# Layer B's attention: 128 joined logits per query, value differences, and the first units laid among eight gate tiles

## The chip, the cores and the metric

The kernel runs on one core of a Trainium2 chip. The metric is the device time of one execution in microseconds (us), lower is better. The kernel before takes 2511.83 us, the median of 3 runs (2511.45 to 2513.24).

## The reference

A trunk of two layers over 2048 positions of width 1024. Layer A projects, attends causally with a forgetting bias, gates and projects out. From its output the keys and values of 4 heads are computed once. Layer B projects 16 query heads and a gate, attends over a window of 128 positions with one learned sink per head, multiplies by silu(gate) and projects out. The change lies in layer B. Its attention, for blocks of 128 queries and a band of 256 keys (the block's own 128 and the 128 before them):

```python
diff = (jnp.arange(WINDOW)[:, None] + WINDOW) - jnp.arange(2 * WINDOW)[None, :]
in_window = (diff >= 0) & (diff < WINDOW)
...
logits = jnp.where(valid[None, :, None, None], logits, -jnp.inf)
sink = jnp.broadcast_to(sinks.astype(jnp.float32).reshape(1, 1, hkv, g, 1, 1), logits.shape[:-1] + (1,))
probs = jax.nn.softmax(jnp.concatenate([logits, sink], axis=-1), axis=-1)[..., :-1]
out = jnp.einsum('bnhgqk,bnkhd->bnqhgd', probs.astype(v.dtype), v_band)
...
h = h + (o * jax.nn.silu(gate)) @ w_out_b[j]
```

Of the 256 keys of the band each query sees exactly 128: query q of a block sees keys 0 to q of its own block and keys q+1 to 127 of the block before.

## The kernel before

Names: PE is the matmul engine, DVE the vector engine, ACT the scalar engine (exp, casts), POOL GpSimd, SP the engine that issues DMAs. SBUF is the working memory, PSUM the memory that matmuls write, in banks of 128x512 float32. The kernel holds a float32 number as a high and a low part, both rounded for PE (float32r), so one product is three matmuls where both sides are split.

What runs before the gate's tiles (the first 1957 us) the change leaves as it was, but for small steps on the constants and the norm factors. Layer B runs `projections` (L618), whose last groups are the gate: 2 groups of 16 tiles. A gate tile is 24 matmuls (L715), a DVE product with a row of norm factors (L721), a Silu on ACT (L722) and a DMA to memory. All tiles use the three b2 banks.

Then comes `attention_b` (L1239): 64 units, one for each of 16 query blocks i and 4 key heads g; a unit has 4 query heads. It is a generator, written as slots. Slot n holds, in this order on PE: `scores` of unit n, `weights_t` of unit n-3 (T_LAG_B), 6 matmuls of the output projection, `values` of unit n-4 (V_LAG_B), and 6 more of the projection (`feed`, O_LAG_B 8, FEED_2 6).

- `scores` (L1273): 8 matmuls give the raw logits of 4 heads, 128 queries by 256 keys, in two b2 banks. DVE adds the band mask and takes the maximum, one instruction for each head (L1290), and writes the masked logits to SBUF. DVE computes the negated maximum nm (L1296) and the sink's part es (L1299); ACT takes four exps, one for each head, 256 wide, which also sum up (L1303), and the exp of es (L1300); DVE adds the sum and es (L1307) and takes the reciprocal (L1308); POOL multiplies the 128x1024 weights by it (L1309).
- `weights_t` (L1314): 8 transposes on PE (flip, L343) into two b2 banks, a cast on ACT to the high part ph (L1327), a DVE subtraction for the low part pl (L1328).
- `values` (L1330): 4 matmuls (L1339): two blocks of values, each with ph and pl, into the one pa bank. ACT copies the lower half (L1346), DVE adds the halves (L1348, two instructions), POOL multiplies by the gate (L1352), ACT casts yh (L1354), DVE subtracts yl (L1355).
- `project` (L1361): 24 matmuls (L1374) for each half of a block's output, into the one pb bank; DVE adds the residual from memory (L1379) and a DMA writes the result. 12 matmuls go to each slot, so the add comes every second slot, and the next group cannot start in the bank before that add is done.

Each engine runs its instructions strictly in its own order, which a scheduler has laid down when the program was built. The lags above set which units stand beside each other in it.

A hook in `layer_b` starts the attention's generator inside the last gate group: the load at tile 8, and the slots of the first 6 units (B_AHEAD) among the last 6 tiles. The weights of the output projection are split into high and low parts by `half` (one half, L1157) and, in slots 6 to 9, by `weights` (L411, ACT cast L447 and DVE subtraction L448).

Of the kernel before, what the change touches and what calls it, by code (L numbers as in the profile page):

```python
# [13 lines left out]
F32R = mybir.dt.float32r  # L14
BF16 = mybir.dt.bfloat16
I32 = mybir.dt.int32
# [61 lines left out]
B_AHEAD = 6  # L78
# [67 lines left out]
class Trunk:  # L146
# [56 lines left out]
    def constants(self):  # L203
# [32 lines left out]
        nc.gpsimd.memset(self.band, 0.0)  # L236
        select(self.band[:, 0, :], self.band[:, 0, :], [[1, P]], -1, -1, NEG)
        select(self.band[:, 1, :], self.band[:, 1, :], [[-1, P]], 0, 1, NEG)
# [163 lines left out]
    def rstd_row(self, r, i):  # L402

        nc = self.nc
        ps = self.ps("pa", [NTB, P])
        self.tc.keep_in_program_order(self.flip(ps, r))
        row = self.sb("ro1", [NTB, P])
        nc.vector.tensor_copy(row, ps)
        nc.sync.dma_start(out=self.d["rr"][i].rearrange("(b t) -> b t", t=P), in_=row)
# [208 lines left out]
    def projections(self, normed, groups, row, later=None, pre=None, hook=None, first=None):  # L618
# [75 lines left out]
        for gi, grp in enumerate(groups):  # L694
# [10 lines left out]
            if "gate" in grp:  # L705
                f0, dst = grp["gate"]
                for ch in range(NCH):
                    rows = self.factor_rows(row, ch)
                    for ft in range(CH // P):
                        if hook is not None and gi == len(groups) - 1:  # L710
                            hook(ch * (CH // P) + ft)
                        ps = self.ps("b2", [P, CH])
# [7 lines left out]
                        sg = self.sb("st", [P, CH])  # L720
                        nc.vector.tensor_tensor(sg, ps, rows, ALU.mult)  # L721
                        nc.scalar.activation(sg, sg, AF.Silu)  # L722
# [434 lines left out]
    def half(self, w, i, tag="wr", **more):  # L1157

        bigs = [self.sb("big", [P, 4, 2, CH], F32R) for _ in range(2)]
        return self.weights(  # L1160
            w, i * CH, CH, tag=tag, **more,
            into=lambda p: (bigs[p // 4][:, p % 4, 0, :], bigs[p // 4][:, p % 4, 1, :]),
        )

# [74 lines left out]
    def attention_b(self, w_out, res, dst):  # L1239
# [4 lines left out]
        blk, st = {}, {}  # L1244
# [19 lines left out]
        def load_v(i):  # L1264

            ts_ = slice(i * P, (i + 1) * P)
            v = self.sb(("qn", "qn", "rows")[i % 3], [P, NKV, P], F32R)
            nc.sync.dma_start(
                out=f_(v), in_=d["vb"][:, ts_, :].rearrange("g t e -> t g e")
            )  # L1270
            g = msg[:, 2 + i % 2, :].rearrange("p (c t) -> p c t", t=P)
            nc.sync.dma_start(out=g, in_=d["gtb"][:, ts_].rearrange("(c p) t -> p c t", p=P))
            blk[i][3:5] = v, g  # L1273

        def scores(u):
# [10 lines left out]
            ms = msg[:, u % 2, :].rearrange("p (h k) -> p h k", k=2 * P)  # L1286
            mx = self.sb("mx", [P, G], bufs=6)
            mask = self.band.rearrange("p b k -> p (b k)")[:, 2 * P - w :]
            for h in range(G):
                nc.vector.tensor_tensor_reduce(  # L1290
                    out=ms[:, h, :w], in0=ps[:, h, :w], in1=mask, scale=1.0, scalar=NEG,
                    op0=ALU.add, op1=ALU.max, accum_out=mx[:, h : h + 1],
                )
# [7 lines left out]
            pf = self.sb("st", [P, G, 2 * P])  # L1301
            for h in range(G):
                nc.scalar.activation(  # L1303
                    pf[:, h, :w], ms[:, h, :w], AF.Exp, bias=nm[:, h : h + 1],
# [5 lines left out]
                pf[:, :, :w], pf[:, :, :w], rs.unsqueeze(2).to_broadcast([P, G, w]), ALU.mult  # L1310
# [3 lines left out]
        def weights_t(u):  # L1314

            i, g = units[u]
            nb = blk[i][5] // P
            pf = st[u]
            ps = self.ps("b2", [P, 2, G, P])
            for b in range(nb):  # L1320
                for h in range(G):
                    self.flip(ps[:, b, h, :], pf[:, h, b * P : (b + 1) * P])
            ph, pl = (
                php[:, 2 * k + u % 2, :].rearrange("p (b h q) -> p b h q", b=2, h=G)
                for k in range(2)
            )
            nc.scalar.copy(ph[:, :nb], ps[:, :nb])  # L1327
            nc.vector.tensor_tensor(pl[:, :nb], ps[:, :nb], f_(ph[:, :nb]), ALU.subtract)  # L1328
            st[u] = (ph, pl)

        def values(u):
            i, g = units[u]
            ph, pl = st.pop(u)
            nb = blk[i][5] // P
            pv = self.ps("pa", [P, G, P])
            for b in range(nb):
                v = blk[i - nb + 1 + b][3]
                for n_, src in enumerate((ph, pl)):
                    nc.tensor.matmul(  # L1339
                        pv.rearrange("p h q -> p (h q)"), v[:, g, :],  # L1340
                        src[:, b].rearrange("p h q -> p (h q)"),
                        start=(b == 0 and n_ == 0), stop=(b == nb - 1 and n_ == 1),
                    )
# [9 lines left out]
            yh, yl = yt[:, i % 2, 0, pr, :], yt[:, i % 2, 1, pr, :]  # L1353
# [3 lines left out]
        W = [None, self.half(w_out, 1)]  # L1357
        msg, php, yt = self.sb("big", [P, 4, 1024]), None, None
# [4 lines left out]
        def project():  # L1363

            for i in range(NTB):
                rows = slice(i * P, (i + 1) * P)
                for nh in range(2) if i else (1, 0):
# [4 lines left out]
                    for p in range(NDT):  # L1372
                        for n_, (y, k) in enumerate(((0, 0), (0, 1), (1, 0))):
                            nc.tensor.matmul(  # L1374
                                ps, yt[:, i % 2, y, p, :], W[nh][k][p],
# [16 lines left out]
        for n in range(N + V_LAG_B):  # L1392
            if n < N:
                scores(n)
            if n == T_LAG_B:
                php = self.sb("big", [P, 4, 1024], F32R)
            if n == V_LAG_B:
                yt = self.sb("big", [P, 2, 2, NDT, P], F32R)
            if B_AHEAD <= n < B_AHEAD + NDT // 2:
                hs, ls = self.weights(w_out, 0, CH, dts=(2 * (n - B_AHEAD), 2 * (n - B_AHEAD) + 1))  # L1400
                W[0] = [W[0][0] + hs, W[0][1] + ls] if W[0] else [hs, ls]
            o = (n - O_LAG_B) * per
            feed(o + FEED_1)
            if 0 <= n - T_LAG_B < N:
# [62 lines left out]
    def layer_b(self, normed, first):  # L1467
# [28 lines left out]
        def hook(n):  # L1496
            if n == NTB - 8 or n >= NTB - B_AHEAD:
# [40 lines left out]
```

## Time and profile before

| | |
|---|---|
| median of 3 runs | 2511.83 us |
| the profiled execution | 2508.55 us |
| its span in the trace | 2506.8 us |
| mean granted PE clock | 0.998 |
| first of the gate's matmuls (L715) | 1957 us |
| nm (L1296) of the units, first to last | 2102.5 to 2470.4 us |
| rest between span and profiled time | 1.75 us |

The trace covers one execution, which was 3.28 us faster than the median. A row of a group reads: line, engine, operation, output and inputs by name, shapes, count, then busy time, the mean of one in ns, and what the engine waited for just before. A row of a timeline reads: start in us, duration, engine, line. In the chain of waits each piece is a stretch of the path that ended last. In a row by windows stand the length of the window and then the busy times and counts of PE, PE's weight loads, DVE, ACT and POOL.

### The profile page before, as it was taken

Reading aid. Unit: us, or ns where it says so; the run is one execution under the profiler, and the core shown is the slowest. Engines: PE = TensorE matmul, PEld = TensorE weight load, DVE = VectorE, ACT = ScalarE, POOL = GpSimd, SP = SyncE. Lnnn points to the kernel's source line nnn. Section 1 sums busy time; section 2 is a strip of 40 time slices with the busy share of each in tenths; the row PEclk is TensorE's granted clock in tenths of the full one; section 3 lists DMA queues with packets and bytes.
Section 4 is the critical chain, followed back from the end, with each engine's and each line's share of the span. In section 5 each row is a group of like instructions: output and inputs, shape, how many; then the busy total and the mean of one; then the engine's idle time right before and its main releaser. Section 6 shows DMA issues by size and latency. Waiting matters only on the chain. (4 is left out here: it accounts for less than half of the span.)

```text
span 2506.8 us, 37302 instructions
## 1 busy us (share of the span) xinstructions
PE 2455.1 (98%) x12256; PEld 2050.1 (82%) x12256; DVE 1766.5 (70%) x4255; ACT 1332.5 (53%) x2574; POOL 919.8 (37%) x611
## 2 busy tenths in 40 slices
PE   8999999999999999999999999999999999899999
PEld 6788899988888777877877778888788888688887
DVE  7656666726888888888888965556666323788885
ACT  5423333415777777877777751145332214777774
POOL 0000000014777777777777752200011000455542
PEclk9999999999999999999999999999999999999999
DMA  5656645687555655565466469965443424755551
GB/s 181 204 158 190 178 148 151 199 268 222 141 149 151 201 142 158 150 186 160 123 202 161 144 186 282 283 216 159 114 131 84 141 91 141 206 168 158 160 143 64
DMA packets 351521, 419.30 MB, mean 167 GB/s; under 512 B 64928, under 2 KB 248256, under 8 KB 345152
## 3 DMA queue, kind: packets, MB, share of 16 engines
q1 hardware_dynamic: 351328, 416.92, 57.3%
q8 instruction: 97, 1.59, 0.3%
q14 instruction: 96, 0.79, 0.1%
HBM read 265.29 MB, written 151.40 MB: 166 GB/s over the span
## 5 line engine op out<-in xcount | busy, mean ns | idle before, releaser
L750 PE MATMUL b<-wh,big 128*128 128x512 f32 (+3 forms) x2560 | 771.6, 375 | 9.2 <-ACT wh L480 8.8
L994 POOL TENSOR_TENSOR big<-st,big 128x1024 fp32r<-128x1024 f32 (+1 forms) x320 | 659.2, 2075 | 276.0 <-ACT big L993 172.0
L750 PEld LDWEIGHTS b<-wh,big 128*128 128x128 f32 x2560 | 472.3, 189 | 80.2 <-ACT wh L480 11.4
L750 PE MATMUL b<-wl,big 128*128 128x512 f32 (+3 forms) x1280 | 474.4, 371 | 1.6 <-DVE wl L481 1.6
L1003 DVE TENSOR_TENSOR ac<-ac,st 128x512 f32<-128x512 f32 (+3 forms) x576 | 355.1, 617 | 53.2 <-ACT st L990 24.5
L990 ACT ACTIVATE st<-sc 128x512 f32<-128x512 f32 (+1 forms) x512 | 274.9, 584 | 158.6 <-PE sc L976 82.5
L1018 PE MATMUL pa<-big 128*128 128x512 f32 (+3 forms) x1280 | 327.1, 370 | 3.2 <-POOL big L994 1.1
L993 ACT CAST big<-st 128x1024 fp32r<-128x1024 f32 (+1 forms) x320 | 295.6, 924 | 7.9
L750 PEld LDWEIGHTS b<-wl,big 128*128 128x128 f32 x1280 | 242.0, 189 | 38.0 <-DVE wl L481 5.5
L1018 PEld LDWEIGHTS pa<-big 128*128 128x128 f32 x1280 | 223.0, 190 | 49.3 <-ACT sq L1026 16.8
L489 ACT ACTIVATE sq<-b,r 128x512 f32<-128x512 f32 (+2 forms) x128 | 77.8, 608 | 302.4 <-PE b L750 299.2
L938 DVE CUSTOM_DVE_ANT_0 mx<-mx,rot 128x128 f32<-128x128 f32 (+3 forms) x240 | 210.5, 877 | 39.3 <-PE mx L927 31.0
L975 PE MATMUL sc<-big 128*128 128x512 f32 (+3 forms) x640 | 231.1, 365 | 1.3 <-DVE st L536 1.1
L976 PE MATMUL sc<-big 67*128 67x512 f32 (+3 forms) x640 | 229.9, 368 | 0.0
L927 PE MATMUL mx<-big 66*128 66x128 f32 (+3 forms) x660 | 192.1, 365 | 11.2 <-DVE mt L938 10.6
L1052 PE MATMUL pb<-wh,wr 128*128 128x512 f32 x488 | 179.3, 399 | 3.8 <-DMA wr<-wg 3.2
L491 DVE TENSOR_REDUCE sm<-sq 128x8 f32<-128x512 f32 (+2 forms) x128 | 74.9, 585 | 139.3 <-ACT sq L489 139.0
L715 PE MATMUL b<-big,wh 128*128 128x512 f32 x512 | 158.3, 390 | 1.4 <-DVE st L721 1.3
L1309 POOL TENSOR_TENSOR st<-st,rs 128x1024 f32<-128x1024 f32 (+1 forms) x64 | 118.4, 1850 | 109.9 <-DVE rs L1308 101.8
L850 POOL MEMSET rot<- 128x1024 bf16 x1 | 1.0, 952 | 421.0 <-PE pb L343 421.0
L927 PEld LDWEIGHTS mx<-big 66*128 66x128 f32 x660 | 113.7, 191 | 50.9 <-DVE mt L938 20.9
L975 PEld LDWEIGHTS sc<-big 128*128 128x128 f32 x640 | 121.6, 190 | 23.1 <-DVE st L536 1.5
(252 smaller groups left out, 4306.4 us busy)
## 6 DMA issues: line engine op xcount, KB each, us to landing
wr<-wg SPq DMA_DIRECT2D x62, 512.0 KB
va<-st SPq DMA_DIRECT2D x32, 512.0 KB
ka<-st SPq DMA_DIRECT2D x64, 256.0 KB
ut<-big SPq DMA_DIRECT2D x16, 1024.0 KB
big<-ka SPq DMA_DIRECT2D x16, 1024.0 KB
big<-qa SPq DMA_DIRECT2D x16, 1024.0 KB
qb<-st SPq DMA_DIRECT2D x64, 256.0 KB
big<-qb SPq DMA_DIRECT2D x16, 1024.0 KB
```

The costliest lines, as they stand in the source:

```text
L715: nc.tensor.matmul(ps, W[k][dt][:, ft * P : (ft + 1) * P], u[ch][:, dt, :], start=(dt == 0 and i == 0), stop=(dt == NDT - 1 and i == 2),)
L750: nc.tensor.matmul(ps[:, :n], u[tb // 4][:, dt, us], W[k][dt], start=(dt == 0 and i == 0), stop=(dt == NDT - 1 and i == 2),)
L927: mm = nc.tensor.matmul(ps[:, b, :wb], qb[:66, i * P : (i + 1) * P], kb[:66, k0 + b * wb : k0 + (b + 1) * wb], start=True, stop=True,)
L938: nc.vector.tensor_tensor_reduce(out=lg, in0=lg, in1=mask, scale=1.0, scalar=NEG, op0=ALU.add, op1=ALU.max, accum_out=f_(o),)
L975: nc.tensor.matmul(o, ka[:, ks], qa[:, qs], start=not (last and n_), stop=False)
L976: nc.tensor.matmul(o, kb[:, ks], qb[:, qs], start=False, stop=not diag)
L990: nc.scalar.activation(pf[:, off : off + w], ps[:, :w], AF.Exp, scale=HD**-0.5)
L993: nc.scalar.copy(ph[:, :tw], pf[:, :tw])
L994: nc.gpsimd.tensor_tensor(pl[:, :tw], pf[:, :tw], f_(ph[:, :tw]), ALU.subtract)
L1003: nc.vector.tensor_tensor(a_, a_, pf[:, off : off + w], ALU.add)
L1018: nc.tensor.matmul(pv[:, q0 : q0 + w], v[:, k, :], src[:, off : off + w], start=(p == 0 and n_ == 0 and i == 0), stop=(last and n_ == 1 an ...
L1052: nc.tensor.matmul(ps, w[:, dt // 2 % 2, wk, dt % 2, :], us[dt][uk], start=(dt == 0 and i == 0), stop=(dt == NDT - 1 and i == 2),)
```

## The change

Each query's 128 visible logits are joined in one tile. DVE's predicated copy (L1294) overwrites, in PSUM, the own block's logit by the previous block's wherever the own key is not visible; a mask of 16-bit ones and zeros says where. One DVE maximum over the 128x4x128 tile (L1296) gives the four maxima. The exps read PSUM and are 128 wide (L1306), POOL's normalise is 128x512 (L1312), a unit has 4 transposes (L348) and halves in the ACT cast (L1328) and the DVE subtraction (L1329). For block 0 there is no previous block, and a mask is added.

With joined weights p, the output is (previous values) x p + (own - previous values) x (p where the own key is visible). So two new POOL products per unit multiply ph and pl by the triangle tri (L1333, 128x512 each) into oh and ol, and once a block `differences` computes own minus previous values: three POOL instructions (L1340 128x512, L1342 and L1345 128x4x64) and an ACT cast (L1344). `values` has 4 matmuls as before.

The gate's Silu becomes Tanh of half the argument: the row of norm factors is halved (L413), ACT writes tanh to PSUM, and one more DVE instruction per tile (L730, 32 tiles) computes (tanh + 1) times the half. The program holds 9 loads of activation tables, and 22 before. Gate tiles alternate between the pb and b2 banks. The load of the attention stands at gate tile 6, and 8 units are laid among the last 8 tiles. The weights of the output projection are loaded and split in eight pieces, in slots 3 to 11.

```diff
-B_AHEAD = 6
+B_AHEAD = 8
+B_LOAD_AT = 6
+B_SPLIT_AT = 4
...
-                        ps = self.ps("b2", [P, CH])
+                        ps = self.ps(("pb", "b2")[ft % 2], [P, CH])
...
-                        sg = self.sb("st", [P, CH])
+                        sg = self.sb("sq", [P, CH])
                         nc.vector.tensor_tensor(sg, ps, rows, ALU.mult)
-                        nc.scalar.activation(sg, sg, AF.Silu)
+                        nc.scalar.activation(ps, sg, AF.Tanh)
+                        nc.vector.scalar_tensor_tensor(sg, ps, 1.0, sg, ALU.add, ALU.mult)
...
+            lg = ps[:, :, w - P : w]
+            if i == 0:
+                m = self.band[:, 0].unsqueeze(1).to_broadcast([P, G, P])
+                nc.vector.tensor_tensor(lg, lg, m, ALU.add)
+            else:
+                m = self.band[:, 1].bitcast(I16).unsqueeze(1).to_broadcast([P, G, P])
+                nc.vector.copy_predicated(lg, m, ps[:, :, :P])
             mx = self.sb("mx", [P, G], bufs=6)
-            for h in range(G):
-                nc.vector.tensor_tensor_reduce(
-                    out=ms[:, h, :w], in0=ps[:, h, :w], in1=mask, scale=1.0, scalar=NEG,
-                    op0=ALU.add, op1=ALU.max, accum_out=mx[:, h : h + 1],
-                )
+            nc.vector.reduce_max(mx, lg, axis=AX.X)
...
-                    pf[:, h, :w], ms[:, h, :w], AF.Exp, bias=nm[:, h : h + 1],
+                    pf[:, h], lg[:, h], AF.Exp, bias=nm[:, h : h + 1],
...
             nc.gpsimd.tensor_tensor(
-                pf[:, :, :w], pf[:, :, :w], rs.unsqueeze(2).to_broadcast([P, G, w]), ALU.mult
+                pf, pf, rs.unsqueeze(2).to_broadcast([P, G, P]), ALU.mult
             )
...
+            for h in range(G):
+                self.flip(ps[:, h, :], pf[:, h])
+            ph, pl, oh, ol = (
+                php[:, u % 2, k, :].rearrange("p (h q) -> p h q", h=G) for k in range(4)
+            )
+            nc.scalar.copy(ph, ps)
+            nc.vector.tensor_tensor(pl, ps, f_(ph), ALU.subtract)
+            if i:
+                own = self.tri.unsqueeze(1).to_broadcast([P, G, P])
+                for o, w in ((oh, ph), (ol, pl)):
+                    nc.gpsimd.tensor_tensor(o, f_(w), own, ALU.mult)
+            st[u] = (ph, pl, oh, ol)
+
+        def differences(i):
+            v, before = f_(blk[i][3]), f_(blk[i - 1][3])
+            t = self.sb("wl", [P, NKV, P])
+            nc.gpsimd.tensor_tensor(t, v, before, ALU.subtract)
+            t_ = t[:, :, :HD]
+            nc.gpsimd.tensor_tensor(t_, t_, t[:, :, HD:], ALU.add)
+            dv = self.sb("wh", [P, NKV, P], F32R)
+            nc.scalar.copy(dv[:, :, :HD], t_)
+            nc.gpsimd.tensor_tensor(dv[:, :, HD:], t_, f_(dv[:, :, :HD]), ALU.subtract)
+            dvs[i] = dv
...
+            if i:
+                v, dv = blk[i - 1][3], dvs[i]
+                terms = ((v, ph), (v, pl), (dv, oh), (dv, ol))
...
+            if 0 <= n - B_SPLIT_AT < NDT:
+                weight_split(n - B_SPLIT_AT)
+            if 0 <= n + 1 - B_SPLIT_AT < NDT:
+                weight_load(n + 1 - B_SPLIT_AT)
...
+            if n % NKV == 1 and NKV < n < N:
+                differences(n // NKV)
...
-            if n == NTB - 8 or n >= NTB - B_AHEAD:
+            if n == B_LOAD_AT or n >= NTB - B_AHEAD:
```

How this moves instructions is seen in the middle of the attention. First PE, from a unit's transposes to the end of its slot (b is a bank of b2 that holds logits or turned weights; pb the projection's bank, pa that of `values`). Before:

```order
L343 MATMUL b_23812<-ident,st 128x128 x8
L1374 MATMUL pb<-big 128x512 x6
L1339 MATMUL pa<-big,rows 128x512 x2
L1339 MATMUL pa<-big,qn 128x512 x2
L1374 MATMUL pb<-big 128x512 x6
```

PE, the same stretch of a slot now:

```order
L348 MATMUL b_23685<-ident,st 128x128 x4
L1428 MATMUL pb<-big,wh 128x512 x2
L1428 MATMUL pb<-big,wl 128x512
L1428 MATMUL pb<-big,wh 128x512 x2
L1428 MATMUL pb<-big,wl 128x512
L1361 MATMUL pa<-big,rows 128x512 x2
L1361 MATMUL pa<-big,wh 128x512 x2
L1428 MATMUL pb<-big,wh 128x512 x2
L1428 MATMUL pb<-big,wl 128x512
L1428 MATMUL pb<-big,wh 128x512 x2
L1428 MATMUL pb<-big,wl 128x512
```

Four transposes are gone; the rest of the slot stands where it stood, with the second half of the value matmuls on dv (wh) in place of a block's values.

On DVE, the stretch around the residual add of the projection, which frees pb (mx, nm, es and rs are the small tiles of the softmax, wr the unit's output, sq the residual). Before:

```order
L1328 TENSOR_TENSOR big<-b_21246,big 128x1024
L1296 SCALAR_TENSOR_TENSOR nm<-mx,nsink 128x4
L1299 TENSOR_TENSOR es<-nm,sink 128x4
L1348 TENSOR_TENSOR wr<-pa,wr 64x256 x2
L1379 TENSOR_TENSOR sq<-pb,sq 128x512
L1290 ISA big,mx<-b_21283,band 128x256
L1290 ISA mx 128x1
L1307 TENSOR_TENSOR rs<-rs,es 128x4
```

DVE, around the residual add now:

```order
L1294 COPY_PREDICATED b_23139<-band,b_23139 128x4x128
L1377 TENSOR_TENSOR big<-wr,big 128x256
L1296 TENSOR_REDUCE mx<-b_23139 128x4
L1329 TENSOR_TENSOR big<-b_23165,big 128x512
L1299 SCALAR_TENSOR_TENSOR nm<-mx,nsink 128x4
L1302 TENSOR_TENSOR es<-nm,sink 128x4
L1310 TENSOR_TENSOR rs<-rs,es 128x4
L1434 TENSOR_TENSOR sq<-pb,sq 128x512
L1311 RECIPROCAL rs<-rs 128x4
L1370 TENSOR_TENSOR wr<-pa,wr 64x256 x2
```

Before, the residual add (L1379) and the value adds (L1348) stood between es and the sum rs (L1307) of the same unit. Now the residual add (L1434), and in every second slot the value adds (L1370), stand behind the sum rs (L1310), which needs the unit's last exp.

On POOL, a stretch of the same part of the program (st is a unit's weights, rs the reciprocal, wr the unit's output, big the tiles of ph, pl, oh and ol, of the gates and of the keys). Before:

```order
L1258 MEMSET big_23509 64x1024
L1309 TENSOR_TENSOR st_22923<-st_22923,rs_22919 128x1024
L1352 TENSOR_TENSOR wr_23024<-wr_23024,big_20008 128x256
L1309 TENSOR_TENSOR st_22994<-st_22994,rs_22990 128x1024
L1352 TENSOR_TENSOR wr_23095<-wr_23095,big_20008 128x256
```

POOL, the same part of the program now:

```order
L1312 TENSOR_TENSOR st_23610<-st_23610,rs_23606 128x512
L1333 TENSOR_TENSOR big_20212<-big_20212,tri_84 128x512 x2
L1312 TENSOR_TENSOR st_23677<-st_23677,rs_23673 128x512
L1340 TENSOR_TENSOR wl_23811<-rows_23720,qn_23460 128x512
L1374 TENSOR_TENSOR wr_23705<-wr_23705,big_19942 128x256
L1333 TENSOR_TENSOR big_20212<-big_20212,tri_84 128x512
L1342 TENSOR_TENSOR wl_23811<-wl_23811 128x4x64
L1333 TENSOR_TENSOR big_20212<-big_20212,tri_84 128x512
L1345 TENSOR_TENSOR wh_23814<-wl_23811,wh_23814 128x4x64
L1374 TENSOR_TENSOR wr_23772<-wr_23772,big_19942 128x256
L1312 TENSOR_TENSOR st_23741<-st_23741,rs_23737 128x512
```

Before, normalise (L1309) and gate product (L1352) alternated. Now each unit has two triangle products (L1333) as well, and once a block the three steps of the value differences (L1340, L1342, L1345) stand between them. A unit's normalise stands directly behind the triangle products of an earlier unit.

96 lines of the change are left out of this document (50 added, 46 removed).

## The prediction

> **What bounds the kernel now.** I read the page's busy times first, then the windows over the last 390 us, the chain of waits there, the groups by line, and last the timelines of DVE and POOL. The page's first row:
>
> ```profile
> PE 2455.1 (98%) x12256; PEld 2050.1 (82%) x12256; DVE 1766.5 (70%) x4255; ACT 1332.5 (53%) x2574; POOL 919.8 (37%) x611
> ```
>
> PE is busy for 98% of the span. The windows say whether that holds in the attention (after the window and its length stand PE, weight loads, DVE, ACT, POOL, each with its count):
>
> ```profile
> 2120.00:2160.00 40.00, 34.08 (x184) 27.73 (x183) 23.02 (x88) 32.46 (x74) 14.18 (x12) 1.00 0.58 168
> 2160.00:2470.00 310.00, 303.38 (x1746) 262.94 (x1745) 263.81 (x918) 223.00 (x666) 156.00 (x122) 1.00 0.55 156
> ```
>
> PE is idle for 5.92 us in the first and 6.62 in the second, 12.5 together. It is a list of single stalls, of which these are three:
>
> ```profile
> 2146.02 0.38 PE L1280 MATMUL b<-big 128*128 128x256 f32 x1 [1.26 <-DVE st L721]
> ...
> 2156.19 1.67 PE L1374 MATMUL pb<-big 128*128 128x512 f32 x6 [1.07 <-ACT big L1354]
> ...
> 2181.49 0.50 PE L1374 MATMUL pb<-wl,big 128*128 128x512 f32 x1 [1.33 <-DVE wl L448]
> ```
>
> They lie where the gate tiles end and the projection's weights are split. Behind them PE runs through, and the chain of waits is PE alone. One slot of it:
>
> ```profile
> 2326.90 1.39 PE pb L1374 x6
> 2328.29 0.12 PE b L1280
> ...
> 2329.24 0.87 PE b L343 x8
> 2330.11 1.39 PE pb L1374 x6
> 2331.50 0.94 PE pa L1339 x4
> 2332.44 1.39 PE pb L1374 x6
> 2333.82 0.12 PE b L1280
> ```
>
> From 2328.29 to 2333.82 is a slot of 5.53 us: 0.95 of logits, 0.87 of 8 transposes, 1.39, 0.94 and 1.39. The 310 us are 56 such slots, in which POOL works 156/56 = 2.8 us, DVE 4.7 and ACT 4.0. POOL stands half idle, and nobody waits for it for long.
>
> **The change, part by part.**
>
> Transposes. 8 become 4: 0.87/2 = 0.435 us less of PE in a slot, 60 units (16 blocks but the first, by 4) make 26 us. PE's own slot is then 5.10. This is a gain only where PE still sets the pace.
>
> DVE and ACT. Their rows:
>
> ```profile
> L1303 ACT ACTIVATE st<-big,nm 128x256 f32<-128x256 f32 x196 | 96.8, 497 | 1.9 <-DVE nm L1296 1.9
> L1290 DVE CUSTOM_DVE_ANT_0 big<-b,band 128x256 f32<-128x256 f32 x196 | 78.2, 419 | 21.0 <-PE b L1283 19.0
> L1328 DVE TENSOR_TENSOR big<-b,big 128x1024 fp32r<-128x1024 f32 x49 | 60.0, 1224 | 0.0
> L1379 DVE TENSOR_TENSOR sq<-pb,sq 128x512 f32<-128x512 f32 x24 | 16.6, 692 | 0.7
> L491 DVE TENSOR_REDUCE sm<-sq 128x8 f32<-128x512 f32 x64 | 43.8, 685 | 84.3 <-ACT sq L489 84.3
> L1303 ACT ACTIVATE st<-big,nm 128x128 f32<-128x128 f32 x16 | 6.2, 391 | 0.0
> ```
>
> Four masked maxima (4 x 0.42 = 1.68) go. A predicated copy and one maximum come. The trace has no predicated copy; its nearest row is L1379, 128x512 with one input from PSUM, 0.69, and I take that; half of it (0.35) and twice it (1.4) are the ends. The maximum is L491's 0.69. The subtraction L1329 is L1379's 0.69 in place of 1.22. So DVE falls by 1.68 + 1.22 - 3 x 0.69 = 0.8, to 3.9 us in a slot; with a copy of 1.4 it is 4.6, still under 5.10. Four exps of 128 save 4 x 0.106 on ACT. Neither engine is the bound by its work.
>
> POOL. Its rows:
>
> ```profile
> L1309 POOL TENSOR_TENSOR st<-st,rs 128x1024 f32<-128x1024 f32 x60 | 114.2, 1904 | 75.6 <-DVE rs L1308 71.9 <-DVE nm L1296 2.3 <-DVE es L1299 1.4
> L1352 POOL TENSOR_TENSOR wr<-wr,big 128x256 f32<-128x256 f32 x64 | 47.8, 747 | 111.5 <-DVE wr L1348 80.3 <-issue 25.6 <-DMA sq<-h 3.6
> L1258 POOL MEMSET big<- 64x1024 f32 x15 | 14.2, 948 | 0.0
> L1309 POOL TENSOR_TENSOR st<-st,rs 128x512 f32<-128x512 f32 x4 | 4.2, 1042 | 34.3 <-DVE rs L1308 29.9 <-ACT st L1303 4.5
> L1184 POOL TENSOR_TENSOR qn<-qn,wh 128x512 f32<-128x512 f32 x3 | 3.9, 1287 | 4.2 <-PE pa L1018 2.7 <-DMA qn<-om 1.5
> ```
>
> The normalise is block 0's row, 1.04. A triangle product reads two tiles of 128x512: between 1.04, where one input is a single number for each row, and 1.29 of L1184, where both stream. The triangle streams too, only its outer step is zero, so I take 1.29. Gate product 0.75; a quarter of the differences, (1.29 + 2 x 0.75)/4 = 0.70; a quarter of the memset, 0.24. The sum is 1.04 + 2 x 1.29 + 0.75 + 0.70 + 0.24 = 5.31 us of POOL per unit, where it was 1.90 + 0.75 + 0.24 = 2.89. That is more than PE's new 5.10 and little less than the old slot. The Trainium skill (GPSIMD Engine Reference, section 3.1, Elementwise) gives a two-input product some 2.6 cycles per element at 1.2 GHz; for 512 that would be an estimated 1.11 without its dispatch, 0.36 less for the pair, and some 20 us less at the end. L1184 was measured here on the same form, so its 1.29 decides.
>
> What a full POOL does to DVE. In the trace before, three places show it; for each, DVE's row and then POOL's:
>
> ```profile
> 2173.37 1.72 DVE L1299 TENSOR_TENSOR es<-nm,sink 128x4 f32<-128x4 f32 x1
> ...
> 2177.36 0.52 DVE L1307 TENSOR_TENSOR rs<-rs,es 128x4 f32<-128x4 f32 x1
> ...
> 2203.31 1.85 DVE L1296 SCALAR_TENSOR_TENSOR nm<-mx,nsink 128x4 f32<-128x4 f32 x1
> ```
>
> ```profile
> 2173.17 1.90 POOL L1309 TENSOR_TENSOR st<-st,rs 128x1024 f32<-128x1024 f32 x1 [2.26 <-DVE nm L1296]
> ...
> 2177.12 0.74 POOL L1352 TENSOR_TENSOR wr<-wr,big 128x256 f32<-128x256 f32 x1 [1.17 <-DVE wr L1348]
> ...
> 2203.22 1.92 POOL L1309 TENSOR_TENSOR st<-st,rs 128x1024 f32<-128x1024 f32 x1 [0.27 <-DVE rs L1308]
> ```
>
> ```profile
> L1299 DVE TENSOR_TENSOR es<-nm,sink 128x4 f32<-128x4 f32 x49 | 7.9, 161 | 1.6
> ```
>
> ```profile
> 2215.83 1.22 DVE L1328 TENSOR_TENSOR big<-b,big 128x1024 fp32r<-128x1024 f32 x1
> ```
>
> ```profile
> 2215.42 1.90 POOL L1309 TENSOR_TENSOR st<-st,rs 128x1024 f32<-128x1024 f32 x1 [1.51 <-DVE rs L1308]
> ```
>
> L1299 usually takes 0.16. At 2173.37 it took 1.72 and ended at 2175.09, right behind POOL's product (2175.07). L1296 ended at 2205.16, POOL's at 2205.14; L1307 at 2177.88, POOL's at 2177.86. So a DVE step whose inputs both lie in SBUF, issued while a POOL product runs, ends only behind that product. Instructions with an input in PSUM show nothing of it (the last two rows: L1328 at its usual 1.22 inside a POOL product). The Trainium skill (SBUF — State Buffer, section Who interferes with whom) states this as an exclusive lock on a shared port, for DVE instructions with two SBUF inputs against GpSimd instructions that read SBUF; by it the sum is the one below, without it the second rival's, and the three places agree with it. Before, POOL runs half the time and DVE's small steps mostly fall into its gaps. Now there are none to fall into, and each unit has four such steps: nm, es, rs and yl.
>
> The loop that follows. nm must come before the exps, the exps before rs, rs before the reciprocal, and that before POOL's normalise. In POOL's order the normalise stands behind the triangle products of an earlier unit, and nothing else can run before it. So nm ends with one product; the next one (1.29) runs beside the exps. From nm to the normalise it takes four exps (4 x 0.39), then rs and the reciprocal (0.16 each) and some handing over, about 2.2. POOL therefore idles 2.2 - 1.29 = 0.9 in a unit: 5.31 + 0.9 = 6.2. Where rs or yl too wait for half a product (0.5 or so), it is 6.7. I take 6.5.
>
> Who pays: in the order now the residual add (L1434), which frees the single pb bank, stands behind rs on DVE. Behind rs are queued that add, the reciprocal and the value adds; PE's next 6 projection matmuls wait for the add, all the rest of PE's order for them. Before, that add stood ahead of rs and waited for nothing but PE. So the round of DVE and POOL becomes PE's slot.
>
> From here 6.5 - 5.53 = 0.97 us in each of the 52 slots from 2182 on, or 50 us.
>
> The first units and the gate. Eight units are laid among gate tiles, and the splits of the weights are smaller. The 12.5 us of stalls stand in this stretch; I let 8 of them go (bounds 0 and 11) and keep 4.5, because the projection's first groups still start there. The table loads:
>
> ```profile
> L722 ACT ACT_TABLE_LOAD x6 | 7.7, 1283 | 7.9 <-issue 4.5 <-DVE st L721 3.3
> ```
>
> That row and L1303's and L1300's loads go, and ACT has air there beside PE, so their worth is inside those 8. Tanh's extra DVE step is 0.69 (L1379's row) on 32 tiles of which each has 24 matmuls of PE to hide it: nothing; without that cover 22 us. The 8 units before the steady part have 4 transposes less each, 8 x 0.435 = 3.5 us. The loads move to tile 6 on SP's queue, ahead of the gates' own stores; they wait for nothing new.
>
> Sum: 50 - 8 - 3.5 = +38.5; with two or three slots more in the pinched part, because the units' tail after the last scores still has POOL's work, **+41 us**. The profiled execution (2508.55) would become 2550, and the median of 2511.83, which lies 3.28 above it, 2553.
>
> **The rivals.**
>
> PE stays the bound (the other side, faster). If POOL's triangle products cost under 1.0 and DVE's steps slip between them, every slot is 5.10: -26 for the transposes and -8 for the stalls, 2478. For it speaks that PE has had 98% so far and that DVE and ACT lose work. It decides where POOL's unit, with its idle time, is under 5.10; 5.31 of work alone speaks against it. Chance 0.14.
>
> No holding: the three places were coincidence, and only the new order acts. POOL's 5.31 and a wait at each normalise of 0 to 0.6 give slots of 5.3 to 5.9, that is -12 to +19, less 11.5: 2488 to 2520, with 2505 the middle. Chance 0.10.
>
> Each hold is worse: all four steps wait for a whole product, as at 2173.37. POOL and DVE then alternate, 5.31 + 4 x 0.4 = 6.9 or more: +71 from the slots, and no stall gone: 2580 and above. Chance 0.12.
>
> The predicated copy is slow: 1.4 on DVE. DVE has 5.10 - 3.9 = 1.2 us to spare and mostly waits for POOL, so this moves the time by less than 10 us; it is inside the forecast.
>
> **How the numbers follow.** The forecast has 0.64, from 2530 (slots of 6.1) to 2570 (6.8), likeliest 2553. The range of 2500 to 2582 leaves out the first rival, a part of the second and the upper part of the third, 0.2 together. What a measurement of this kernel can tell from no change is about 0.2%, 5 us. Faster by more: 0.14 and 0.03 of the second rival, 0.17. Within: 0.05. Slower: 0.78.
>
> **What would show it.** In the profile of the changed kernel POOL is busy over 75% of the steady part, with L1333 at about 1290 ns. The mean of nm (L1299), es, rs and yl is two to five times that of before. PE shows idle time of 1 to 2 us before L1428, released by DVE sq L1434, in every second slot, and slots of 13 us in pairs. L1294 and L1296 are near 0.69. The stalls around the last gate tiles are fewer. I am wrong if nm stays at its usual 0.16 beside a running L1333, if PE is idle for under 0.3 us in a slot, or if L1333 takes under 1.0.

## The result, and the profile after

The changed kernel takes 2594.91 us (median of 4 runs, 2592.67 to 2595.53), the kernel before 2511.65 beside it: a ratio of 1.0337, 95% interval 1.0325 to 1.0349. It is slower by 83 us. The forecast had the side right (slower), but 41 us where 83 came, and the time lies above its range.

The page's busy times of the changed kernel:

```profile
PE 2472.5 (95%) x12016; PEld 2048.4 (79%) x12016; DVE 1836.0 (71%) x3896; ACT 1269.7 (49%) x2568; POOL 1066.3 (41%) x775
```

The windows show the middle of the attention (after the length stand PE, weight loads, DVE, ACT and POOL, then the granted clock):

```profile
2300.00:2400.00 100.00, 83.03 (x386) 67.56 (x385) 77.57 (x141) 44.27 (x165) 73.05 (x70) 0.88 0.41 121
```

PE, which ran without a pause here before, is idle for 17% of the time. POOL has gone from half to 73%; no engine is full. The timeline of PE gives the length of a slot, by the first logits matmul of unit 20 and that of unit 60:

```profile
2236.68 0.28 PE L1280 MATMUL b<-big 128*128 128x256 f32 x1
...
2528.20 0.28 PE L1280 MATMUL b<-big 128*128 128x256 f32 x1
```

(2528.20 - 2236.68)/40 = 7.29 us, where the kernel before has 5.52 by the same measure. Every slot costs 1.77 us more. What PE waits for between 2200 and 2560 us (total, times, longest):

```profile
PE pb L1428 <- DVE sq L1434: 57.3, 25, 2.8
PE pa L1361 <- DVE wr L1370: 6.1, 5, 1.5
```

So PE waits for the residual add, as forecast. Why DVE comes late stands in its groups from 2300 to 2550 us, some 34 units:

```profile
L1377 DVE TENSOR_TENSOR big<-wr,big 128x256 fp32r<-128x256 f32 x18 | 25.7, 1426 | 7.6 <-ACT big L1376 7.6
L1296 DVE TENSOR_REDUCE mx<-b 128x4 f32<-128x512 f32 x35 | 23.7, 678 | 0.0
L1294 DVE COPY_PREDICATED b<-band,b 128x512 f32<-128x512 int16 x34 | 23.0, 676 | 0.5 <-PE b L1283 0.5
L1377 DVE TENSOR_TENSOR wl<-wr,wh 128x256 fp32r<-128x256 f32 x17 | 22.5, 1326 | 8.3 <-ACT wh L1376 8.3
L1302 DVE TENSOR_TENSOR es<-nm,sink 128x4 f32<-128x4 f32 x34 | 20.4, 601 | 1.2
L1299 DVE SCALAR_TENSOR_TENSOR nm<-mx,nsink 128x4 f32<-128x4 f32 x35 | 18.4, 527 | 0.6
L1310 DVE TENSOR_TENSOR rs<-rs,es 128x4 f32<-128x4 f32 x34 | 7.3, 215 | 34.6 <-ACT st L1306 34.6
```

The predicated copy (0.68) and the maximum (0.68) cost what was estimated. But nm takes 0.53 in the mean (its shortest is 0.15), es 0.60 (0.16), yl (L1377) 1.38 (0.39), rs 0.22 (0.16). By these differences the four are held for 1.85 us in a unit. And in front of rs DVE stands idle for 34.6/34 = 1.0 us a unit, for the exps. POOL's groups of the same window:

```profile
L1333 POOL TENSOR_TENSOR big<-big,tri 128x512 fp32r<-128x512 f32 x70 | 93.1, 1336 | 12.9 <-DVE nm L1299 9.8 <-DVE es L1302 1.9
L1312 POOL TENSOR_TENSOR st<-st,rs 128x512 f32<-128x512 f32 x34 | 35.3, 1039 | 35.1 <-DVE rs L1311 35.1
```

The triangle products are at 1.34 in the mean (median 1.29), the normalise at 1.04, and POOL waits 1.0 us a unit for the reciprocal. What a hold looks like, DVE's row and then POOL's:

```profile
2409.11 2.66 DVE L1377 TENSOR_TENSOR wl<-wr,wh 128x256 fp32r<-128x256 f32 x1
```

```profile
2409.19 1.03 POOL L1312 TENSOR_TENSOR st<-st,rs 128x512 f32<-128x512 f32 x1
2410.19 1.29 POOL L1333 TENSOR_TENSOR big<-big,tri 128x512 fp32r<-128x512 f32 x1
```

yl ended at 2411.77, 0.29 after the second product: two products that followed each other without a gap held it. All 7 of the 35 yl steps of this window that took over 2.6 us had started beside POOL's memset (L1258), ahead of both products. The other 28 met a running product and ended behind that one, though POOL's next product followed it at once.

### The profile page after: what moved, and what is told of

It reads as the page before. It is cut to its first block, busy times and chain, and to the rows that moved or that the text cites. A ratio compares the mean times of both kernels' runs of the same rounds, so it can differ in the third digit from the quotient of the medians.

```text
span 2593.3 us, 36540 instructions
## 1 busy us (share of the span) xinstructions
PE 2472.5 (95%) x12016; PEld 2048.4 (79%) x12016; DVE 1836.0 (71%) x3896; ACT 1269.7 (49%) x2568; POOL 1066.3 (41%) x775
## 4 chain that ended last, share of the span: by engine, by line
PE 39%; DVE 9%; ACT 4%; DMA 3%; POOL 3%; issue 2%; SPq 0%; POOLq 0%; ACTq 0%; DVEq 0%
PE b L758 9%; PE b L1221 5%; PE pa L1026 4%; PE pb L1060 3%; PE b L721 3%; PE pb L721 3%; ACT st L1306 2%; PE pb L1428 2%; PE mx L935 2%; PE sc L984 2%; PE sc L983 2%; DVE es L1302 1%; DVE big L1377 1%; DVE mx L1296 1%; DVE wl L1377 1%
## 5 line engine op out<-in xcount | busy, mean ns | idle before, releaser
L1333 POOL TENSOR_TENSOR big<-big,tri 128x512 fp32r<-128x512 f32 x120 | 159.6, 1336 | 24.3 <-DVE nm L1299 16.3
L1428 PE MATMUL pb<-big 128*128 128x512 f32 x384 | 114.1, 437 | 35.9 <-DVE sq L1434 35.4
```

The source lines that it names most:

```text
L1428: nc.tensor.matmul(ps, yt(i, y, slice(p, p + 1))[:, 0, :], W[nh][p // 4][:, k, p % 4, :], start=(p == 0 and n_ == 0), stop=(p == NDT - 1 a ...
```

## The experiments

Theory 1: POOL's products hold those DVE steps whose inputs both lie in SBUF, and the round of DVE and POOL is PE's slot. Its rivals: A, the order alone (the residual add behind rs); B, POOL's work alone, without holds; C, PE's clock, which falls behind a wait; D, DVE's own work; E, the joined logits' chain. "Against before" is the median less that of the kernel before, run beside it on the same chip. The slot is taken as above.

| kernel | median us | against before | ratio (95%) | slot us |
|---|---|---|---|---|
| changed | 2594.91 | +83.3 | 1.0337 (1.0325 to 1.0349) | 7.29 |
| e1_no_triangles | 2522.52 | +13.7 | 1.0053 (1.0033 to 1.0073) | 5.96 |
| e2_memsets | 2540.56 | +31.7 | 1.0125 (1.0101 to 1.0149) | 6.31 |
| e3_triangles_from_psum | 2509.11 | +0.3 | 1.0003 (0.9993 to 1.0012) | 5.74 |
| e4_warm | 2604.16 | +95.3 | 1.0379 (1.0358 to 1.0399) | 7.31 |
| e5_add_first | 2585.91 | +76.8 | 1.0311 (1.0293 to 1.0330) | 7.10 |
| e6_no_triangles_add_first | 2522.30 | +13.2 | 1.0058 (1.0039 to 1.0076) | 6.00 |
| e7_psum_and_max_in_psum | 2502.89 | -6.3 | 0.9977 (0.9968 to 0.9986) | 5.43 |
| b1_before_two_products | 2573.16 | +65.4 | 1.0267 (1.0237 to 1.0297) | 6.33 |
| b2_before_memsets | 2509.95 | +2.2 | 1.0015 (1.0002 to 1.0028) | 5.52 |
| e8_no_triangles_sum_later | 2497.83 | -9.9 | 0.9951 (0.9935 to 0.9968) | 5.62 |
| e8_full_sum_later | 2555.02 | +47.3 | 1.0195 (1.0158 to 1.0231) | 6.60 |
| e9_psum_sum_later | 2502.04 | -8.3 | 0.9968 (0.9957 to 0.9978) | 5.52 |

### Without the triangle products, and with memsets in their place

```diff
-                for o, w in ((oh, ph), (ol, pl)):
-                    nc.gpsimd.tensor_tensor(o, f_(w), own, ALU.mult)
+                oh, ol = ph, pl
```

> The changed kernel without its two triangle products (L1333); ph and pl stand in their place in the last two value matmuls, so own keys that a query must not see get a weight. POOL's work falls from 5.31 to 2.73 us a unit. Theory 1 (POOL's products hold DVE's small steps, and PE's slot is the round of the two, 7.3 us measured): slots of 5.2 to 5.5, 2495 to 2520 us. Rival A (the order alone: the residual add stands behind rs and so behind the exps, whatever POOL does): the order of these is the same, so 2570 to 2595. Rival B (POOL's work alone, without holds): 2495 to 2520 too; the next kernel tells it apart.

```diff
-                for o, w in ((oh, ph), (ol, pl)):
-                    nc.gpsimd.tensor_tensor(o, f_(w), own, ALU.mult)
+                for k in (2, 2, 3):
+                    nc.gpsimd.memset(f_(php[:, u % 2, k : 4, :]), 0.0)
```

> The two triangle products of each unit replaced by three memsets of the same tiles, which leaves the own block's part out of the output. A memset reads nothing from SBUF, and beside one DVE's steps ran at their usual times before. 0.95 + 0.95 + 0.5 = 2.4 us of POOL where 2.58 were: POOL is as busy, but holds DVE no longer. Theory 1 (the holds): 2495 to 2525 us, close to the kernel without the products. Rival B (POOL's work and its queue, without holds): 2570 to 2595, close to the changed kernel. Rival A (order alone): 2570 to 2595.

Without the products 70 us of the 83 go: the two products are the main cost, and rival A (2570 to 2595) is out. The window of the changed kernel that stands above, now without the products:

```profile
2300.00:2400.00 100.00, 88.16 (x474) 74.34 (x473) 71.89 (x175) 53.80 (x204) 45.09 (x52) 1.00 0.53 155
```

DVE is busy for 71.89 of 100 us in slots of 5.96, which is 4.3 us a slot. In the changed kernel it is 77.57 in slots of 7.29, or 5.65. So DVE's busy time falls by as much as the slot (1.33 us), and its idle time stays (1.6 to 1.7).

With memsets POOL is as full (79.5 of 100 us), and yet 52 us go. yl and nm in that kernel, from 2200 to 2460 us:

```profile
L1376 DVE TENSOR_TENSOR big<-wr,big 128x256 fp32r<-128x256 f32 x21 | 15.8, 754 | 16.1 <-ACT big L1375 16.1
L1299 DVE SCALAR_TENSOR_TENSOR nm<-mx,nsink 128x4 f32<-128x4 f32 x41 | 8.5, 206 | 0.7
```

nm is back at 0.21, yl at 0.75 to 0.79 (one row for each of its two tiles). The four steps together are held for 0.5 us a unit, as in e1, where the changed kernel has 1.85. So 52 of the 83 us go with the holds of the triangle products. Another 18 (31.7 - 13.7) stay with a POOL that is full; rival B had POOL's work as the whole. Whether these 18 are POOL's time or PE's clock (0.95 in e2's window from 2300 to 2400 us, 1.00 in e1's) isn't separated. Both kernels miss what theory 1 gave them (2495 to 2520 and 2495 to 2525), though: +14 is left with no triangle product at all, where the first rival of the forecast had 34 less than before. e1's row of rs shows one part of it, from 2200 to 2460 us:

```profile
L1310 DVE TENSOR_TENSOR rs<-rs,es 128x4 f32<-128x4 f32 x44 | 7.4, 167 | 48.0 <-ACT st L1306 48.0
```

DVE, 72% busy, stands for 1.1 us a unit at rs until the exps are done.

### The same load on the kernel before

```diff
+            for _ in range(2):
+                own = pf[:, :, :P]
+                nc.gpsimd.tensor_tensor(
+                    own, own, self.ones.unsqueeze(1).to_broadcast([P, G, P]), ALU.mult
+                )
             st[u] = pf
```

> The kernel before, with nothing of the change, and two more POOL products a unit (128x512 each, the own half of the weights times one, in place, behind the normalise); the output is the same. POOL has 2.89 + 2.58 = 5.47 us in a slot of 5.53. Theory 1 (POOL's products hold DVE's steps with two SBUF inputs): nm, es, rs and yl are held here too, though nothing of the joined logits is in it: slots of 6.2 to 7.0, 2550 to 2590 us. Rival E (the joined logits' own chain of DVE and ACT makes the time, and POOL's products matter only because the value matmuls wait for them): 2508 to 2520.

```diff
+            for _ in range(2):
+                nc.gpsimd.memset(ms, 0.0)
+            nc.gpsimd.memset(ms[:, :2], 0.0)
             st[u] = pf
```

> The kernel before with three memsets a unit in place of those products (0.95 + 0.95 + 0.52 = 2.42 us, over masked logits that have been used), which read nothing from SBUF; the output is the same. POOL is as full. Theory 1: no holds, 2508 to 2525 us. If a full POOL is the cause, whether it reads or not: 2550 to 2590.

The windows from 2230 to 2460 us, with products and then with memsets:

```profile
2230.00:2460.00 230.00, 203.70 (x1119) 173.46 (x1117) 195.31 (x581) 143.98 (x422) 188.36 (x149) 0.97 0.50 140
```

```profile
2230.00:2460.00 230.00, 230.00 (x1332) 201.23 (x1331) 193.43 (x690) 166.54 (x499) 214.32 (x219) 1.00 0.56 157
```

With memsets POOL is busy for 93% of the time and PE for all of it: +2 us. With products POOL is busy for 82%, PE for 89%: +65 us. The step es, in the first and in the second:

```profile
L1299 DVE TENSOR_TENSOR es<-nm,sink 128x4 f32<-128x4 f32 x36 | 35.1, 976 | 1.1
```

```profile
L1299 DVE TENSOR_TENSOR es<-nm,sink 128x4 f32<-128x4 f32 x42 | 6.8, 163 | 1.5
```

DVE's busy time is 5.4 us in a slot of 6.33 with products, and 4.6 in one of 5.52 with memsets: that is most of the 0.8 us between the slots, and es alone is held for 0.81. Nothing of the change is in these kernels, so rival E is out as the whole of it. The products, unlike the memsets, also lie on the way from rs to the transposes. But from 2190 to 2500 us PE's weight loads wait there for POOL for only 1.1 us. A POOL that is full costs nothing here; one that reads SBUF while DVE needs two SBUF inputs costs 63 us. The Trainium skill (SBUF — State Buffer, section Who interferes with whom) says that such DVE instructions contend with GpSimd instructions that read SBUF and not with those that only write it; the 976 and 163 ns agree.

### PE kept busy in its wait

```diff
-            ps = self.ps("b2", [P, 2, G, P])[:, 0]
+            both = self.ps("b2", [P, 2, G, P])
+            ps = both[:, 0]
...
+            if u % 2 and u + T_LAG_B > O_LAG_B:
+                wm = W[1][0]
+                for _ in range(6):
+                    nc.tensor.matmul(
+                        both[:, 1].rearrange("p h q -> p (h q)"), wm[:, 0, 0, :P], wm[:, 0, 0, :],
+                        start=True, stop=True,
+                    )
```

> The changed kernel with 6 matmuls of no use (128x512, results never read) behind the transposes of every second unit, just ahead of the projection group that waits for the residual add. PE's idle time there falls from 1.8 to 2.8 us to 0.4 to 1.4. Rival C (PE's granted clock falls after such a wait, and the slow matmuls behind it, 427 ns apart instead of 231, some 31 us in all, lengthen the round): the clock stays at 1.0 and the time falls by 10 to 30 us, 2565 to 2585. Theory 1 alone (PE is late for others' sake; its slow matmuls lie inside the round): between no change and +30 us, since 46 us of matmuls are added, 2595 to 2625.

```profile
2230.00:2460.00 230.00, 194.09 (x974) 153.54 (x973) 147.64 (x331) 104.31 (x390) 163.14 (x158) 1.00 0.43 129
```

The clock stays at 1.00, where the changed kernel has 0.90 in the same window, and the slot is as long as before (7.31). The time lies in the bounds for added matmuls without a price for the clock; of the 10 to 30 us that rival C wanted back, none is seen. But the test isn't clean. The 29 added groups are 29 x 6 x 0.231 = 40 us of matmuls (not 46), most of it in waits. And the scheduler set DVE's steps in another order: nm (0.15) and yl (0.45) are no longer held, and the four holds together are 0.8 us a unit where the changed kernel has 1.9 in this window. DVE's idle time rose instead, from 1.6 to 2.6 us a slot, and 41 us of it in this window stand before yl, where the changed kernel has 14. So holds that go do not by themselves shorten the round, and what the clock costs by itself stays open.

### The order on DVE

In e5 the residual add is issued ahead of the unit's sum rs, by an edge of issue order. For this the sum, the reciprocal and the normalise stand later in the program, and the scheduler then set the value adds ahead of rs too. e6 is the same without the triangle products. In the two e8 kernels rs is issued behind the next unit's predicated copy, in the same way.

```diff
-            nc.vector.tensor_tensor(rs, rs, es, ALU.add)
+            total_ = nc.vector.tensor_tensor(rs, rs, es, ALU.add)
+            if added:
+                self.tc.add_manual_dep(
+                    total_.ins, added[0].ins.name,
...
+                    reason="residual add first",
+                )
```

> The changed kernel, everything computed, with one thing changed in DVE's order: the residual add (which frees pb) is issued ahead of the same unit's sum rs, as it was before the change, and no longer behind it. Measured so far: 2594.9 us, and 2522.5 without triangle products in the order as it is. Theory 1 with the order as a term of its own (holds first, order second): PE no longer waits for the add, but POOL's and DVE's round stays: slots of 6.4 to 7.2, 2550 to 2590. Rival A (order alone): 2485 to 2520. If the order weighs nothing beside the holds: 2590 to 2600.

> No triangle products (ph and pl in their place, so own keys that a query must not see get a weight), and the residual add ahead of rs. In the kernel without the products PE waited 39 us for that add, in 29 stalls. If that is the order's doing: the 39 us go, 2483 to 2495 us, slots of 5.1 to 5.3. If the add is only the place where a round of DVE shows: 2505 to 2520.

Putting the add first takes 7 us off the full kernel, which lies in theory 1's range, and nothing off the one without products, which comes out 2 us above both ranges. PE's waits in e5, from 2190 to 2500 us:

```profile
PE b L348 <- DVE big L1343: 28.0, 22, 1.9
PE pb L1442 <- DVE sq L1448: 13.8, 19, 1.8
```

PE waits for the add for 13.8 us, where the changed kernel has 50.0 in the same stretch, and now for 28.0 at the transposes, for the subtraction pl of an earlier unit. What DVE waits for in e6, from 2200 to 2460 us:

```profile
DVE wr L1382 <- ACT wr L1380: 31.6, 22, 1.4
DVE rs L1316 <- ACT st L1307: 13.2, 21, 0.7
```

The wait has moved to the value adds, whose copy stands behind the same exps on ACT: 45 us where it was 48. The add is only the place where the round shows.

```diff
-                nc.vector.copy_predicated(lg, m, ps[:, :, :P])
+                copied[:] = [nc.vector.copy_predicated(lg, m, ps[:, :, :P])]
...
+            if 0 < n <= N:
+                normalise(n - 1)
```

> The changed kernel without triangle products (own keys that a query must not see get a weight) took 2522 us, slots of 5.96; DVE there was busy for 72% and stood 48 us at the sum rs, waiting for the unit's exps. Here rs is issued behind the next unit's predicated copy, so DVE has other work while ACT takes the exps. If that wait is what is left beside the holds: slots of 5.1 to 5.5, 2480 to 2505 us. If the wait only moves to another instruction, as with the residual add: 2515 to 2525.

> The changed kernel, everything computed, with only that order changed: rs behind the next unit's predicated copy. Theory 1 (the round of DVE is its own work, the holds and its waits for the exps, 1.0 us a slot): the holds stay, the wait goes: slots of 6.2 to 6.8, 2540 to 2575. If the wait moves elsewhere: 2580 to 2600. If the order is the main cause and not the holds: 2490 to 2515.

Both times lie in the first of their ranges, the slot of the one without products (5.62) does not: 24 us (13.7 + 9.9) go without the products, 36 (83.3 - 47.3) with them. DVE no longer waits at rs. But here too a wait has come up at the value adds, whose copy stands behind the exps on ACT. From 2230 to 2460 us, in the full kernel and then without the products:

```profile
DVE wr L1384 <- ACT wr L1382: 36.7, 17, 2.4
```

```profile
DVE wr L1382 <- ACT wr L1380: 59.3, 21, 5.1
```

In the full kernel DVE's idle time falls from 1.6 to 1.1 us a slot, for it waits no longer before yl either. Without the products the idle time stays at 1.6, and what falls is the time of yl (0.42 in the mean, 0.84 in e1), which is held no longer. So the order is a term of its own, of 24 to 36 us. That the wait for the exps alone makes it is not shown. The other holds stay; in the full kernel, from 2230 to 2460 us:

```profile
L1303 DVE TENSOR_TENSOR es<-nm,sink 128x4 f32<-128x4 f32 x36 | 30.4, 844 | 0.6
L1316 DVE TENSOR_TENSOR rs<-rs,es 128x4 f32<-128x4 f32 x35 | 20.7, 590 | 0.5
```

With rs later, the products cost 47.3 + 9.9 = 57 us.

### The triangle taken from PSUM

```diff
-            ps = self.ps("b2", [P, 2, G, P])[:, 0]
+            both = self.ps("b2", [P, 2, G, P])
+            ps, own_ps = both[:, 0], both[:, 1]
...
-                for o, w in ((oh, ph), (ol, pl)):
-                    nc.gpsimd.tensor_tensor(o, f_(w), own, ALU.mult)
+                nc.vector.tensor_tensor(own_ps, ps, own, ALU.mult)
+                nc.scalar.copy(oh, own_ps)
+                nc.vector.tensor_tensor(ol, own_ps, f_(oh), ALU.subtract)
```

> Everything is computed. The turned weights are multiplied by the triangle on DVE from PSUM into the free second bank of the same tile, ACT casts oh, DVE subtracts ol: 2 x 0.69 more on DVE with one input in PSUM each, 0.58 more on ACT, 2.58 less on POOL. Theory 1: POOL's holds are rare again, DVE has 3.9 + 1.4 = 5.3 us in a slot by full durations and some 4.7 by starts; slots of 5.1 to 5.4, 2485 to 2515 us, and faster than before if PE sets the pace. Rival A (order alone): 2570 to 2600. Rival D (DVE's own work becomes the bound): 5.3 to 5.8, 2510 to 2540.

```profile
L1299 DVE SCALAR_TENSOR_TENSOR nm<-mx,nsink 128x4 f32<-128x4 f32 x46 | 31.4, 682 | 0.0
```

All but 0.3 of the 83 us go, with everything computed. DVE is now the bound (254.78 of 260 us busy, slots of 5.74), as rival D had it; the time lies in theory 1's range and 0.9 us below D's. nm is still held for 0.53 by what POOL has left: 24 of these 46 steps start within 0.1 us behind the start of a normalise, and each takes 1.0. So its maximum goes to PSUM:

```diff
-            mx = self.sb("mx", [P, G], bufs=6)
+            mx = ps[:, 0, :G] if i else self.sb("mx", [P, G], bufs=6)
```

> Triangle products from PSUM on DVE as in the kernel that took 2509 us, and the four maxima are written to a dead part of the logits' PSUM bank (blocks 1 to 15), so that nm has one input in SBUF and one in PSUM. In that kernel DVE was busy for 97% of the time, nm took 0.68 in the mean and yl 0.70 for 0.39. Theory 1 (the hold goes with the second SBUF input): nm falls to 0.15 to 0.2, DVE has 0.5 us less in a slot, slots of 5.2 to 5.5, 2485 to 2502 us. If a hold has another reason than the two SBUF inputs: nm stays at 0.68 and the time at 2505 to 2513.

```profile
L1299 DVE SCALAR_TENSOR_TENSOR nm<-b,nsink 128x4 f32<-128x4 f32 x48 | 7.2, 149 | 0.0
L1302 DVE TENSOR_TENSOR es<-nm,sink 128x4 f32<-128x4 f32 x47 | 13.8, 294 | 0.0
```

nm is at 0.15: with one input in PSUM it isn't held, although 23 of the 48 steps start within 0.1 us behind the start of a normalise, as in e3. Of the 0.53 of hold, 0.15 passes to es behind it, which takes 0.29 where it took 0.14 in e3. The kernel takes 2502.89 us, 0.9 above the range of theory 1 (slot 5.43, inside its range), and is 6.3 us faster than the kernel before.

The last kernel is e7 with rs behind the next unit's predicated copy, as in e8.

> Triangle products from PSUM and maxima in PSUM, as in the kernel that took 2502.9 us (PE busy for 97% there, DVE for 95%), and the sum rs behind the next unit's predicated copy as well. Everything is computed. If DVE's wait for the exps still cost something there (8.6 us before rs in 310): 2490 to 2500 us. If its extra work on the triangle had filled that wait already, as the chain of waits (98% PE) says: 2500 to 2508, no gain.

The later sum brings nothing clear on top (0.9968 and 0.9977, with overlapping intervals). nm is at 0.15 there too, but es at 0.59, held by the normalise. In e7 PE is busy for 225.48 of 230 us, and has 68% of the chain of waits there; the 98% of the expectation hold for 2400 to 2422 us alone. Its slot is 5.43 and not 5.10. In e7 the scheduler set value matmuls directly behind the transposes, and once in two slots the chain of waits has

```profile
2410.11 0.64 PE b L348 x4
2410.76 0.05 issue
2410.81 1.19 PE pa L1363 x4
```

0.64 and 1.19 where 0.435 and 0.94 were reckoned. That the new order is why they take longer is not shown.

## Why the prediction was wrong

**Transposes, DVE's and ACT's work: right.** L1294 at 0.68 and L1296 at 0.68 against 0.69 each; neither engine is the bound by its work. The slots in which PE waits for nothing take 5.1 us, as reckoned.

**POOL: right.** L1333 at 1.29 (median), L1312 at 1.04, the differences at 1.29 and 0.75 to 0.90; POOL is busy for 73% of 7.29 = 5.3 us a slot against 5.31.

**What a full POOL does to DVE: right in kind.** b1 and b2 show it on the kernel before, and e7 shows for nm that one input in PSUM ends it. Two of the signs named were missed: POOL is busy for 73% and not over 75, and rs takes 1.3 times its usual time, where two to five were named (nm, es and yl take 3.5 to 3.8 times).

**The loop: this step failed.** "POOL therefore idles 2.2 - 1.29 = 0.9 in a unit: 5.31 + 0.9 = 6.2." With some part of a hold more, 6.5 was taken; the slot is 7.29. The round was closed on POOL, with little more than one hold in it. It closes on DVE, which runs in order, with ACT's exps: from 2230 to 2460 us DVE has half of the chain of waits, ACT a fifth, POOL an eighth. In a slot DVE has about 3.8 us of its own work (77.57 of 100 us busy is 5.65 a slot, less 1.85 of holds), 1.85 of holds, and 1.64 idle, mostly before rs (1.0) and yl (0.45). Of the holds yl alone has 0.99, for it mostly meets a product at its start and at times two; nm has 0.37 and es 0.44, both of them and not nm alone. POOL idles 2.0 us a slot, not 0.9: 1.0 before the normalise, the rest before the gate product (0.5) and the triangle products (0.4), each time for DVE. The difference of 0.8 us in the 47 slots from unit 16 to unit 63 is 37 us.

**Who pays: half right.** PE waits at the residual add (57.3 us). But its place behind rs is not why: in e5 it stands first, and 7 of 83 us go. More weight has rs standing right behind es, where DVE is idle for 1.0 us a unit while ACT works: with rs later 36 us go (e8), though a part of the wait only moves. The prediction had those exps in its loop as POOL's waiting time and did not see them as DVE's.

**First units and gate: failed.** The -11.5 us did not come. At the first logits of unit 16 the changed kernel is 1.0 us behind the kernel before (2206.26 against 2205.29), while e1 is 6.2 ahead, e3 7.7 and e8 without products 12.3. So the gain is there where the triangle products are off POOL. In the changed kernel the old stalls go but for 0.5 us, and others come, 9.8 us of them at the residual add, of which the longest is

```profile
2167.31 2.93 PE L1428 MATMUL pb<-big 128*128 128x512 f32 x6 [5.71 <-DVE sq L1434]
```

The sum as measured in the traces: 1.0 at unit 16, 83.6 more by unit 63, 2 in the tail: 86.5 in the span, where -11.5 + 50 + 2.5 = 41 was forecast.

**The rivals.** "No holding" is out by b1 and b2. "Each hold is worse" (6.9 or more, no stall gone, 2580 and above) came nearest to the time, although es and rs are not held by a whole product each. PE stays the bound only once the triangle leaves POOL.

Still open: why a yl that has started beside a memset is then held by two products and otherwise by one; what PE's lower clock costs by itself; and what the 14 us of e1 are made of. e8 without products shows one more part. Once a block ACT's cast of the value differences (L1356 there) stands ahead of a unit's exps and waits for POOL, for 31.4 us in 230 and up to 4.1 at a time. Ahead of that, POOL waits for 19.3 us for the loads of the values from memory. These waits pass on to the exps, to ACT's copy and so to the 59 us at the value adds.

## What to carry to other kernels

Before giving POOL more products, count the DVE steps with two SBUF inputs that will run beside them; a [128, 4] step of 0.16 us can cost a whole product (1.2 us in b1), and a step with one input in PSUM, or beside a memset, was free of it here. When POOL fills up, sum the round on the engine that runs in order and is held (own work, holds, waits), not on the one that holds. An instruction that other engines wait for is not sped up by being first in its order if the wait only passes to the next one.

## What the runs showed of the hardware

PE's clock fell behind waits of under 3 us. Two groups of the same six matmuls in the changed kernel:

```profile
2401.88 2.93 PE L1428 MATMUL pb<-big 128*128 128x512 f32 x6 [2.82 <-DVE sq L1434]
...
2405.74 1.52 PE L1428 MATMUL pb<-big 128*128 128x512 f32 x6
```

Behind a wait of 2.82 us the six take 2.93, otherwise 1.52, and the granted clock from 2400 to 2500 us is 0.91. The Trainium skill (TensorE: Matmul & The Clock Gate, Part 1) has the clock at half rate after an idle window of some 3.4 us; here a wait of 2.82 us was enough, and one of 1.84 at 2209.66, where the six take 2.24. The length of the wait alone does not decide it: behind 1.88 us at 2268.93 the six take 1.66, and e1, with waits of 1.81 in every fourth slot, has a clock of 1.00 from 2300 to 2400 us. In e4 the clock stayed up and the time did not fall, but that test was not clean.
